# Small tiles allocated together, and fillers so that TensorE's operands start at multiples of 512 bytes

## The chip, the cores and the metric

The kernel runs on one core of one Trainium2 chip. The metric is the device time of one execution in microseconds (us). Of the kernel before, three timed runs are given, with a median of 2034.71 us.

## What is computed

One decoder layer on x of 1024 tokens by 1024 channels: a SwiGLU block (`ffn1`), a token mixer, a second SwiGLU block (`ffn2`) and a final RMS norm. A vector c gives nine sets of 1024 modulation numbers ("mods"), which shift, scale and gate the three blocks:

```python
mod = silu(c) @ w_ada + b_ada;  sh1, sc1, g1, sh2, sc2, g2, sh3, sc3, g3 = split(mod, 9)
x = x + 0.5 * g1 * swiglu(modulate(rms_norm(x), sh1, sc1))      # w_gate, w_up: 1024 x 2816; w_down: 2816 x 1024
x = x + g2 * token_mixer(modulate(rms_norm(x), sh2, sc2))       # w_in 1024 x 4112, SSD heads, pooling, w_out 2048 x 1024
x = x + 0.5 * g3 * swiglu(modulate(rms_norm(x), sh3, sc3))
return rms_norm(x)
```

Everything is float32 outside the chip.

## The kernel before

**The matmul that nearly all time goes into.** Both operands of a large product are split into a high and a low part of type fp32r (`split` at L117 for activations, `prep` at L141 for weights: a rounded copy on ScalarE, the remainder by a subtraction on VectorE). Each product is three matmuls, in `mmw` (L203 to L208): high weights with high activations, high weights with low activations, low weights with high activations. In each, 128 x 128 weights are loaded (the stationary operand) and 512 columns of activations stream past (the moving operand). Every matmul loads its weights anew, also L207, whose weights are those of L206.

**Stages.** `ffn1.phase1` (gate and up products, in Strassen-like combinations), `ffn1.phase2` (down product), two halves of the mixer (`mixer_half(0)` and `(1)`), `ffn2.phase1`, `ffn2.phase2`, and the final norm. In the profiled execution the mixer runs from about 700 to about 1300 us. In it smaller float32 matmuls (128 or 256 columns, L1000 to L1084) ride between the large ones. Weights come in blocks of 128 x 512: SyncE's queue loads them, ScalarE and VectorE split them ahead of use, and a block's buffer is free again when TensorE has read it (`use`, L161; six buffers of kind `w`). The compute engines run their own instruction streams in order; a planner of the tile framework orders the instructions and sets the semaphores.

**Where tiles lie.** A partition of the on-chip memory is filled from both ends. On the left are the constants, up to byte 1152, the pool `sb`, which lives for the whole kernel, and above it the pools of the stage (`ffn1`/`ffn2`, `mixA`, `mix`). On the right, downwards from byte 229344, are the stage's other pools (`ffnB`, `ph2`, `hid`). Within a pool the tiles lie one after another in the order in which they are first asked for, and each is rounded up to 32 bytes. A tile with a tag and `bufs=n` takes n places at once. So a tile of one column (`mod0` to `mod71`, `epsc`, `warm`) takes 32 bytes, and all that comes after is moved by as much. 229344 is 480 more than a multiple of 512, and most tiles of the right are multiples of 512 long. From this the start of each operand of the fp32r matmuls follows. Here it is as the remainder after division by 512 (steps inside a tile, 512 or 2048 bytes, don't change it):

| operand | pool | remainder |
|---|---|---|
| weights `w` (six buffers, from byte 56640) | sb, left | 320 |
| weights `wo` (four buffers) | hid, right | 480 |
| weights `w0` (first group of an ffn) | ffnB, right | 480 |
| `h`, first half in an ffn | ffn, left | 416 |
| `h`, second half and combinations in an ffn | ffnB, right | 480 |
| `h` in the mixer (from byte 103136) | mixA, left | 224 |
| `tw` (spilled products as moving operand) | ph2, right | 480 |
| `yss`, `pl`, `dp` (mixer outputs) | hid, right | 480 |
| `w` as moving operand (first of seven parts of phase 2) | sb, left | 320 |
| `dtw`, 32 or 16 columns of weights, with `h` of the mixer | mixA, left | 224, 352, 480 and 96 |

The trace writes an operand's tile without its number, and `w0` as `w`.

**The tiles that the change touches.** `vec` (parameter columns, L79), `vb` (L94), `epsc` (L106), `warm` (L110), one tile `mod{j}` for each of 72 modulation columns (L622), `aexp` (L865), `halo` and `uhalo` (L876, L877). `ada` (L621 to L634) makes one modulation column: VectorE multiplies a row block by c and accumulates into the column (L623), and ScalarE finishes it in place (L633). Columns 0 to 15 are made at the start; the other 56 during `ffn1.phase1`, one at every second step of the combinations (L837 to L840), and they are read from `ffn1.phase2` on.

Of the kernel before, what the change touches and what calls it, by code (L numbers as in the profile page):

```python
# [7 lines left out]
F32 = mybir.dt.float32  # L8
F32R = mybir.dt.float32r
AF = mybir.ActivationFunctionType  # L10
# [4 lines left out]
P = 128  # L15
# [3 lines left out]
KD = D // P  # L19
# [26 lines left out]
def hybrid_layer(ctx: ExitStack, tc: tile.TileContext, xT, c_bc, wada, vecs, cst,  # L46
                 gu1, dn1, win, wdt, poolw, wout, gu2, dn2, outT):
    nc = tc.nc

    sb = ctx.enter_context(tc.tile_pool(name="sb", bufs=1, side="left"))  # L50
# [25 lines left out]
    cur["t2"] = (cur["ffn"], 9)  # L76


    vec = sb.tile([P, NV], F32, name="vec")  # L79
    cbc = cur["ffn"].tile([P, D], F32, name="cbc", tag="cbc", bufs=1)  # L80
    crow = sb.tile([1, D], F32, name="crow", tag="raw", bufs=4)
    nc.sync.dma_start(out=crow, in_=c_bc)
# [8 lines left out]
    load_x(0)  # L91
    nc.sync.dma_start(out=vec, in_=vecs)
    ones = sb.tile([P, P], F32, name="ones")
    vb = sb.tile([P, 5 * KD], F32, name="vb")  # L94

    def bias_columns():
        for i, (m, n) in enumerate(((1, V_N1), (4, V_NM), (7, V_N2), (2, None), (8, None))):
# [5 lines left out]
                                               op1=ALU.mult)  # L103

    nc.vector.memset(ones, 1.0)
    epsc = sb.tile([P, 1], F32, name="epsc")  # L106
    nc.vector.memset(epsc, EPS)

    def warm_ln():
        t = sb.tile([P, 1], F32, name="warm", tag="warm", bufs=2)  # L110
        i = nc.scalar.activation(out=t, in_=epsc, func=AF.Sqrt)
        tc.keep_in_program_order(i)

# [496 lines left out]
    mods = {}  # L610
# [8 lines left out]
        return raw  # L619

    def ada(j, raw):  # L621
        acc = sb.tile([P, 1], F32, name=f"mod{j}")  # L622
        nc.vector.scalar_tensor_tensor(out=raw, in0=raw, scalar=1.0, in1=cbc, op0=ALU.mult,  # L623
                                       op1=ALU.mult, accum_out=acc)
        m = j // KD
        k = j % KD
        i = {1: 0, 4: 1, 7: 2, 2: 3, 8: 4}.get(m)
        scale = 1.0
        bias = vec[:, V_BADA + j:V_BADA + j + 1]
        if i is not None:  # L630
            bias = vb[:, i * KD + k:i * KD + k + 1]
            scale = 0.5 if i > 2 else vec[:, (V_N1, V_NM, V_N2)[i] + k:(V_N1, V_NM, V_N2)[i] + k + 1]
        nc.scalar.activation(out=acc, in_=acc, func=AF.Identity, scale=scale, bias=bias)  # L633
        mods[j] = acc  # L634


    def rstd(psb, inv_n, n=HT):
# [131 lines left out]
    with tc.manual_schedule(engines={mybir.EngineType.Activation, mybir.EngineType.DVE}):  # L769
# [4 lines left out]
        with tc.manual_schedule(engines={mybir.EngineType.SP}):  # L774
# [5 lines left out]
            ada_pair(3)  # L780
        n1[0].stat.add_pairs([xt[d][0] for d in range(KD)], cb2)
        warm_ln()
        bias_columns()
        for j in (8, 0):
            ada(j, raws[j])
# [16 lines left out]
    for k in range(1, KD):  # L802
        for j in (8 + k, k):
            ada(j, raws[j])
        n1[0].mk(k)
        for b in stream[state["emitted"]:min(14, state["emitted"] + 2)]:
            b.prep()
            state["emitted"] += 1
# [13 lines left out]
    def side1(where, k):  # L822
        if where == "p0":
            if 2 <= k <= 5:
                with tc.high_priority(150):
                    i = 2 * k - 4
                    n1[1].stat.add_pair(i, KD, [xt[i][1], xt[i + 1][1]])
                    if k == 5:
                        n1[1].stat.fin_pairs()
        elif where == "s" and k < 5:  # L830
            for d in ((0, 1), (2, 3), (4, 5), (6,), (7,))[k]:
                n1[1].mk(d)
        elif where == "p1":
            ffn1.spread(k)
        elif where == "s" and 6 <= k < 14:
            ffn1.spread(k + 2)
        elif where == "c" and k >= 14:  # L837
            if ada_next[0] < 72 and k % 2 == 0:
                ada(ada_next[0], ada_raw(ada_next[0]))
                ada_next[0] += 1  # L840
# [19 lines left out]
    mA = cur["mixA"]  # L860
# [1 line left out]
    trs = mA.tile([P, P], F32, name="trs")  # L862
    ident = mA.tile([P, P], F32, name="ident")
    icnt = mA.tile([P, 16], F32, name="icnt")
    aexp = mA.tile([P, 64], F32, name="aexp")  # L865
    dtw = mA.tile([P, KD, 32], F32R, name="dtw")
    open_pool("ph2", "ph2", "right")
    cur["t2"] = (mA, 8)
# [4 lines left out]
    open_pool("hid", "hidp", "right")  # L873
    open_pool("mix", "mix", "left")
    mp = cur["mix"]
    halo = sb.tile([P, 16, 3], F32, name="halo")  # L876
    uhalo = sb.tile([P, KD, 15], F32, name="uhalo")  # L877
    spers = mp.tile([P, G, 2 * P], F32, name="spers")

    def small(nm):  # L880
# [474 lines left out]
```

## Time and profile before

| | |
|---|---|
| three timed runs | 2037.25, 2034.71 and 2033.18 us |
| profiled execution | 2036.55 us, of it 2034.6 us from the first to the last instruction |
| TensorE matmul / weight load busy | 1992.8 us (98%) / 1590.1 us (78%) |
| VectorE / ScalarE / GpSimd busy | 1564.5 us (77%) / 1010.3 us (50%) / 0.2 us |
| DMA | 331.40 MB, mean 163 GB/s |

A matmul's own duration in the trace (some 0.39 us) is longer than the distance from its start to the start of the next, because matmuls overlap in the engine. The cost of one in a row without waits is that distance. A window's count of instructions takes in each that overlaps the window.

### The profile page before, as it was taken

To read this page: it belongs to the slowest core of one execution; us is meant where nothing else is said; L and a number is where in the kernel's file an instruction comes from. 1 tells how busy PE (TensorE), PEld (TensorE's weight loads), DVE (VectorE), ACT (ScalarE), POOL (GpSimd) and SP (SyncE) were. 2 spreads that over 40 slices of the span, in tenths; PEclk is the share of its full clock that TensorE was granted. 3 is DMA by queue.
4 is the path that set the end of the run, shared out by engine and by line. 5 is a ranking of instruction groups with operands and counts; after the bars stand their busy time and mean duration, and the time that the engine had idled before them with its cause. 6 is when DMAs were issued, how large, how long until landed. Compare 5 with 4: busy or idle time off the path is not lost.

```text
span 2034.6 us, 25195 instructions
## 1 busy us (share of the span) xinstructions
PE 1992.8 (98%) x8768; PEld 1590.1 (78%) x8768; DVE 1564.5 (77%) x2559; ACT 1010.3 (50%) x1761; POOL 0.2 (0%) x4
## 2 busy tenths in 40 slices
PE   7999999999999999999999999999999999999996
PEld 4788888887888688888878887768888888878885
DVE  7977887875878867888967998798665565568877
ACT  5744444443444587654467763465434333344442
POOL 0000000000000000000000000000000000000000
PEclk8999999999999999999999999999999999999998
DMA  8365555555887433332332232334332222278783
GB/s 318 103 238 202 191 202 191 194 194 191 298 308 245 145 113 104 126 103 98 115 130 94 94 130 73 97 129 156 136 119 89 102 107 102 83 261 299 234 281 119
DMA packets 155009, 331.40 MB, mean 163 GB/s; under 512 B 16897, under 2 KB 27905, under 8 KB 153858
## 3 DMA queue, kind: packets, MB, share of 16 engines
q1 hardware_dynamic: 154882, 329.80, 47.7%
q8 instruction: 68, 1.11, 0.2%
q14 instruction: 59, 0.48, 0.1%
HBM read 280.91 MB, written 48.82 MB: 162 GB/s over the span
## 4 chain that ended last, share of the span: by engine, by line
PE 82%; DVE 8%; DMA 7%; ACT 1%; issue 1%; SPq 1%; DVEq 0%; ACTq 0%
PE pb L206 26%; PE pb L207 26%; PE pb L208 26%; DMA dw<-in_dn_dram 3%; DMA dth<-sp 2%; DVE w L151 1%; DVE dw L115 1%; PE pb L1084 1%; DVE x L521 1%; DMA araw<-in_wada_dram 1%; DVE ry L642 1%; DVE tw L151 1%; PE pb L1049 1%; PE pb L1078 1%; DVE sq L696 1%
## 5 line engine op out<-in xcount | busy, mean ns | idle before, releaser
L206 PE MATMUL pb<-h,w 128*128 128x512 f32 x1768 | 707.9, 401 | 11.7 <-ACT w L150 11.7
L207 PE MATMUL pb<-h,w 128*128 128x512 f32 x1768 | 702.4, 397 | 0.0
L208 PE MATMUL pb<-h,w 128*128 128x512 f32 x1768 | 701.5, 397 | 0.0
L206 PEld LDWEIGHTS pb<-h,w 128*128 128x128 f32 x1768 | 333.7, 189 | 97.3 <-ACT w L150 15.0
L208 PEld LDWEIGHTS pb<-h,w 128*128 128x128 f32 x1768 | 333.4, 189 | 83.2 <-issue 1.1
L207 PEld LDWEIGHTS pb<-h,w 128*128 128x128 f32 x1768 | 334.1, 189 | 79.7 <-issue 0.7
L151 DVE TENSOR_TENSOR w<-wraw,w 128x512 fp32r<-128x512 f32 x327 | 220.8, 685 | 96.2 <-ACT w L150 95.5
L150 ACT CAST w<-wraw 128x512 fp32r<-128x512 f32 x327 | 200.5, 619 | 181.5 <-PE pb L208 110.6
L206 PE MATMUL pb<-tw,w 128*128 128x512 f32 (+1 forms) x540 | 212.7, 394 | 3.6 <-DVE x L548 3.6
L207 PE MATMUL pb<-tw,w 128*128 128x512 f32 (+1 forms) x540 | 212.1, 393 | 0.0
L208 PE MATMUL pb<-tw,w 128*128 128x512 f32 (+1 forms) x540 | 211.7, 392 | 0.0
L151 DVE TENSOR_TENSOR w<-ws,w 128x512 fp32r<-128x512 f32 x163 | 111.4, 686 | 63.2 <-ACT w L150 63.0
L150 ACT CAST w<-ws 128x512 fp32r<-128x512 f32 x163 | 101.0, 621 | 86.6 <-PE pb L208 82.2
L150 ACT CAST tw<-dth 128x512 fp32r<-128x512 f32 x132 | 81.8, 620 | 118.4 <-DMA dth<-sp 118.2
L150 ACT CAST w<-dw 128x512 fp32r<-128x512 f32 x154 | 94.9, 618 | 73.5 <-DVE dw L115 37.3
L206 PEld LDWEIGHTS pb<-tw,w 128*128 128x128 f32 x540 | 102.2, 189 | 28.1 <-DVE x L548 4.0
L207 PEld LDWEIGHTS pb<-tw,w 128*128 128x128 f32 x540 | 102.2, 189 | 24.2 <-issue 0.5
L208 PEld LDWEIGHTS pb<-tw,w 128*128 128x128 f32 x540 | 102.2, 189 | 23.8
L151 DVE TENSOR_TENSOR w<-dw,w 128x512 fp32r<-128x512 f32 x154 | 105.0, 685 | 14.8 <-ACT w L150 14.6
L151 DVE TENSOR_TENSOR tw<-dth,tw 128x512 fp32r<-128x512 f32 x132 | 90.0, 686 | 30.2 <-ACT tw L150 28.7
L623 DVE SCALAR_TENSOR_TENSOR araw<-araw,cbc 128x1024 f32<-128x1024 f32 x72 | 87.6, 1221 | 30.3 <-DMA araw<-in_wada_dram 29.9
L115 DVE TENSOR_TENSOR dw<-dw 128x512 f32<-128x512 f32 x110 | 75.5, 687 | 33.4 <-DMA dw<-in_dn_dram 32.6
(217 smaller groups left out, 2466.9 us busy)
## 6 DMA issues: line engine op xcount, KB each, us to landing
dw<-in_dn_dram SPq DMA_DIRECT2D x264, 256.0 KB, 4.4
dth<-sp SPq DMA_DIRECT2D x154, 256.0 KB, 4.5
wraw<-in_gu_dram SPq DMA_DIRECT2D x76, 512.0 KB, 3.6
araw<-in_wada_dram SPq DMA_DIRECT2D x72, 512.0 KB, 3.6
wraw<-in_win_dram SPq DMA_DIRECT2D x64, 512.0 KB, 3.4
wraw<-in_wout_dram SPq DMA_DIRECT2D x64, 256.0 KB, 2.7
sp<-u SPq DMA_DIRECT2D x57, 256.0 KB, 2.0
sp<-x SPq DMA_DIRECT2D x57, 256.0 KB, 2.1
```

The source lines that it names most:

```text
L115: nc.vector.tensor_tensor(out=out, in0=a, in1=b, op=op)
L150: nc.scalar.copy(out=self.w[:, 0, :], in_=self.src)
L151: nc.vector.tensor_tensor(out=self.w[:, 1, :], in0=self.src, in1=self.w[:, 0, :].bitcast(F32), op=ALU.subtract)
L206: nc.tensor.matmul(out=out, lhsT=whi, rhs=act[:, 0, c], start=start, stop=False, skip_group_check=True)
L207: nc.tensor.matmul(out=out, lhsT=whi, rhs=act[:, 1, c], start=False, stop=False, skip_group_check=True)
L208: nc.tensor.matmul(out=out, lhsT=wlo, rhs=act[:, 0, c], start=False, stop=stop, skip_group_check=True)
L521: nc.vector.scalar_tensor_tensor(out=xt[d][hf], in0=src, scalar=g[d], in1=xt[d][hf], op0=ALU.mult, op1=ALU.add)
L623: nc.vector.scalar_tensor_tensor(out=raw, in0=raw, scalar=1.0, in1=cbc, op0=ALU.mult, op1=ALU.mult, accum_out=acc)
L642: nc.vector.reciprocal(out=y, in_=y)
L696: nc.vector.tensor_tensor(out=q, in0=q, in1=self.acc, op=ALU.add)
L1049: nc.tensor.matmul(out=b[:, ci * 256:(ci + 1) * 256], lhsT=self.bt[:, c * P:(c + 1) * P], rhs=self.xds[:, c, :], start=True, stop=True)
L1078: nc.tensor.matmul(out=bo[:, s], lhsT=self.prev[:, c, j * P:(j + 1) * P], rhs=cT[:, s], start=True, stop=True)
```

## The change

Small tiles are asked for at the start, one behind another: `vec`, `vb`, `epsc`, `warm`, 16 columns `mod0` to `mod15`, seven tiles of eight columns for the other 56 modulation columns, four accumulators `macc`, `halo` and `uhalo`. With their 32-byte roundings they take 1152 + 160 + 32 + 64 + 512 + 224 + 128 + 192 + 480 = 2944 bytes (`warm` is asked for with 16 columns, one used). From byte 1152 that reaches byte 4096. On the right a pool `edge` with one tile `spare` of 480 bytes lies at the end. `aexp` is asked for with 112 columns, 64 used. Columns 16 to 71 are accumulated in one of the four `macc` tiles in turn, and ScalarE writes the finished column into a column of a shared tile.

```diff
     vec = sb.tile([P, NV], F32, name="vec")
+    vb = sb.tile([P, 5 * KD], F32, name="vb")
+    epsc = sb.tile([P, 1], F32, name="epsc")
+    warm = [sb.tile([P, 16], F32, name="warm")[:, :1]]
+    mod_first = [sb.tile([P, 1], F32, name=f"mod{j}") for j in range(16)]
+    mod_rest = [sb.tile([P, KD], F32, name=f"mods{m}") for m in range(2, 9)]
+    macc = [sb.tile([P, 1], F32, name=f"macc{i}") for i in range(4)]
+    halo = sb.tile([P, 16, 3], F32, name="halo")
+    uhalo = sb.tile([P, KD, 15], F32, name="uhalo")
+    edge = ctx.enter_context(tc.tile_pool(name="edge", bufs=1, side="right"))
+    spare = edge.tile([P, 120], F32, name="spare")
+    nc.gpsimd.memset(spare, 0.0)
...
-    vb = sb.tile([P, 5 * KD], F32, name="vb")
...
-    epsc = sb.tile([P, 1], F32, name="epsc")
...
-        t = sb.tile([P, 1], F32, name="warm", tag="warm", bufs=2)
+        t = warm.pop()
...
-        acc = sb.tile([P, 1], F32, name=f"mod{j}")
+        out = acc = mod_first[j] if j < 16 else macc[j % 4]
+        if j >= 16:
+            out = mod_rest[j // KD - 2][:, j % KD:j % KD + 1]
...
-        nc.scalar.activation(out=acc, in_=acc, func=AF.Identity, scale=scale, bias=bias)
-        mods[j] = acc
+        nc.scalar.activation(out=out, in_=acc, func=AF.Identity, scale=scale, bias=bias)
+        mods[j] = out
...
-    aexp = mA.tile([P, 64], F32, name="aexp")
+    aexp = mA.tile([P, 112], F32, name="aexp")[:, :64]
...
-    halo = sb.tile([P, 16, 3], F32, name="halo")
-    uhalo = sb.tile([P, KD, 15], F32, name="uhalo")
```

## Rows read from the trace of the kernel before

**Rows 1.** The page: busy time of TensorE; the chain that ended last, by engine.

```profile
PE 1992.8 (98%) x8768; PEld 1590.1 (78%) x8768; DVE 1564.5 (77%) x2559; ACT 1010.3 (50%) x1761; POOL 0.2 (0%) x4
PE 82%; DVE 8%; DMA 7%; ACT 1%; issue 1%; SPq 1%; DVEq 0%; ACTq 0%
```

**Rows 2.** Busy time (count) of each engine by window, granted clock, DMA share, GB/s.

```profile
200.00:300.00 100.00, 100.00 (x429) 80.41 (x429) 81.28 (x133) 43.45 (x85) 0.00 (x0) 1.00 0.57 199
...
1100.00:1200.00 100.00, 100.00 (x533) 81.75 (x532) 89.68 (x151) 78.06 (x132) 0.00 (x0) 1.00 0.38 124
...
1300.00:1400.00 100.00, 95.17 (x388) 73.39 (x387) 87.96 (x134) 60.20 (x102) 0.00 (x0) 0.97 0.33 110
```

**Rows 3.** Timeline of TensorE, 1000 to 1027 us: start, duration, line, output and inputs.

```profile
1000.59 0.40 PE L206 MATMUL pb<-pl,wo 128*128 128x512 f32 x1
...
1011.28 0.39 PE L208 MATMUL pb<-pl,wo 128*128 128x512 f32 x1
1011.51 0.39 PE L206 MATMUL pb<-pl,w 128*128 128x512 f32 x1
...
1022.52 0.40 PE L208 MATMUL pb<-pl,w 128*128 128x512 f32 x1
1022.75 0.39 PE L896 MATMUL pb<-h,dtw 128*32 128x512 f32 x1
...
1026.46 0.40 PE L206 MATMUL pb<-h,w 128*128 128x512 f32 x1
```

**Rows 4.** Timeline of TensorE in phase 2 of ffn1, first part.

```profile
496.15 0.39 PE L207 MATMUL pb<-w 128*128 128x512 f32 x1
...
511.79 0.39 PE L207 MATMUL pb<-w 128*128 128x512 f32 x1
```

**Rows 5.** Matmul groups by line and shape: count, busy us, mean ns, idle before.

```profile
L206 PE MATMUL pb<-h,w 128*128 128x512 f32 x1768 | 707.9, 401 | 11.7 <-ACT w L150 11.7
...
L206 PE MATMUL pb<-tw,w 128*128 128x512 f32 x516 | 205.4, 398 | 0.0
...
L206 PE MATMUL pb<-pl,w 128*128 128x512 f32 x96 | 37.6, 405 | 0.0
...
L206 PE MATMUL pb<-w 128*128 128x512 f32 x88 | 34.5, 392 | 0.9 <-ACT w L150 0.9
...
L206 PE MATMUL pb<-yss,w 128*128 128x512 f32 x64 | 25.7, 402 | 0.0
...
L206 PE MATMUL pb<-yss,wo 128*128 128x512 f32 x64 | 25.3, 396 | 0.0
...
L206 PE MATMUL pb<-dp,w 128*128 128x512 f32 x32 | 12.8, 400 | 0.0
...
L206 PE MATMUL pb<-pl,wo 128*128 128x512 f32 x32 | 12.5, 390 | 0.0
...
L789 PE MATMUL pb<-sq,ones 128*128 128x512 f32 x12 | 5.3, 593 | 0.0
```

**Rows 6.** What TensorE waited for: us in total, times, longest.

```profile
PE pb L206 <- ACT w L150: 12.7, 6, 8.1
```

**Rows 7.** Splitting of a weight block, groups by line and shape.

```profile
L151 DVE TENSOR_TENSOR w<-wraw,w 128x512 fp32r<-128x512 f32 x327 | 220.8, 685 | 96.2 <-ACT w L150 95.5
...
L150 ACT CAST w<-wraw 128x512 fp32r<-128x512 f32 x327 | 200.5, 619 | 181.5 <-PE pb L208 110.6 <-issue 50.9 <-DMA wraw<-in_gu_dram 11.3
```

**Rows 8.** Busy time by window where DMA and VectorE are fullest.

```profile
560.00:580.00 20.00, 20.00 (x87) 16.06 (x86) 15.32 (x26) 12.62 (x23) 0.00 (x0) 1.00 0.96 332
...
1120.00:1140.00 20.00, 20.00 (x102) 16.22 (x101) 19.91 (x40) 14.53 (x23) 0.00 (x0) 1.00 0.29 93
```

**Rows 9.** Timeline of TensorE at the start: four float32 matmuls, one behind another.

```profile
16.95 1.88 PE L789 MATMUL pb<-sq,ones 128*128 128x512 f32 x4
```

**Rows 10.** A modulation column's two instructions, groups by line and shape.

```profile
L623 DVE SCALAR_TENSOR_TENSOR araw<-araw,cbc 128x1024 f32<-128x1024 f32 x72 | 87.6, 1221 | 30.3 <-DMA araw<-in_wada_dram 29.9
...
L633 ACT ACTIVATE mod<-mod,vec 128x1 f32<-128x1 f32 x32 | 9.4, 294 | 18.5 <-DVE araw L623 18.4
```

## The prediction

> **What bounds the kernel now.** I read the page's busy times first. TensorE is busy for 98% of the span with 8768 matmuls and as many weight loads [rows 1], while VectorE has 77% and ScalarE 50%, so less work on either of those would buy little. The chain that ended last says the same: 82% of it is TensorE, 8% VectorE, 7% DMA. Next come the windows [rows 2]. From 200 to 300 us TensorE has no idle time, the granted clock is 1.00 (2.4 GHz, the upper of the two levels), and 429 matmuls fall in the window. An instruction that only overlaps the window's edge is counted too, and one lasts some 0.39 us, so the distance from start to start is (100 + 0.39) / 429 = 0.2340 us. Nothing waits there, so this distance is the kernel's price, and what would change it must be in the matmuls themselves.
>
> So I looked for places where the same matmul runs at another distance, and the timeline has one [rows 3]. A single call of `down` runs 48 matmuls with weights from `wo` and then 48 with weights from `w`. Line, shape, moving tiles (`pl`) and clock are the same. The first 48 go from 1000.59 to 1011.28 us: 47 steps, 227.4 ns each. The other 48 go from 1011.51 to 1022.52 us: 47 steps, 234.3 ns each. The reader is to see that only the place of the weights differs: `wo` and `pl` both start at remainder 480, `w` at 320. The second such place is the first part of phase 2, where weights and moving operand both lie in `w` (320 and 320): 69 steps from 496.15 to 511.79 us, 226.7 ns each [rows 4]. My reading is that a step costs 226.7 ns where both operands start at the same remainder modulo 512, and 234 ns where they don't.
>
> **The change part by part.** *Addresses.* By the sizes in the change the small tiles end at byte 4096, so `raw`, `x`, `ones`, `ry` and `w` behind them start at multiples of 512, and `ffn`, `mixA` and `mix` too, since `sb` is then 161 x 512 bytes long. On the right 229344 - 480 = 228864 = 447 x 512. In `mixA` 64 + 448 bytes (`icnt`, `aexp`) make 512, so `dtw` and `h` start at multiples as well. All fp32r operands of L206 to L208 then have remainder 0. It isn't quite "every operand": `ut` (L1127) is 2112 bytes long and shares its tag with the `gt` tiles, so these still go up in steps of 64, and some float32 operands behind them follow. That concerns the small matmuls only, and I count nothing for it.
>
> *What it saves.* Pairs with unequal remainders: `h`,`w` 1768, `tw`,`w` 516, `pl`,`w` 96, `yss`,`w` 64, `dp`,`w` 32 for one line of three, so 3 x 2476 = 7428 matmuls [rows 5]. Equal already: `w` alone 88, `yss`,`wo` 64, `pl`,`wo` 32, so 3 x 184 = 552 [rows 5]. With 234.0 ns [rows 2] going to 226.7 ns [rows 4], 7.3 ns x 7428 = 54.2 us. The 72 matmuls of 256 columns near the end and the 32 with `dtw` add under 0.5 us, and I leave them out.
>
> *What of it is not handed on.* Where TensorE waits for another engine, a faster row of matmuls before it only makes the wait longer. From 1300 to 1400 us 388 matmuls stand where 429 would fit [rows 2], and the waits for `w` copies add up to 12.7 us over the run [rows 6]. I count some 400 matmuls ahead of such waits (about 150 in that window, the rest at the start, between ffn1 and the mixer, and at the end; an estimate from these rows): 400 x 7.3 ns = 3 us. The gain is then 51 us. Its ends: 54 us if all is handed on, and some 41 us if the stretches below give back 10 us.
>
> *Who is late next.* The weights are split ahead of TensorE, and what ends ScalarE's idle time before a copy is mostly TensorE giving a buffer free (110.6 of 181.5 us [rows 7]), so preparation waits for TensorE, not the reverse. Its cost per block (619 ns on ScalarE, 685 ns on VectorE [rows 7]) stands against 12 matmuls, 2.72 us at the new distance. Two places have little room: DMA's share is 0.96 from 560 to 580 us, and VectorE is busy for 19.91 of 20 us from 1120 to 1140 us [rows 8]. In both TensorE had no idle time, and the window of 100 us around the second has VectorE at 89.68% [rows 2]. Speeding TensorE up by 3% asks for 92%. That fits, with some waits where bursts meet. If this cover fails in the mixer (some 600 us, 3% of which are 18 us, less where small matmuls stand), about half of that, 10 us, goes; that is the lower end above.
>
> *The small tiles.* The same instructions run. A column's accumulation on VectorE takes 1.22 us and ScalarE's finish 0.29 us [rows 10], unchanged; only the target of the latter moves. Sharing four accumulators adds a wait: the accumulation of column j must come after ScalarE's read for column j - 4. VectorE's other work is queued behind it, and TensorE waits for that in the end. But columns are made at every second step of the combinations, so four of them span some twenty microseconds, and ScalarE's instruction follows the accumulation directly. Cost 0. If each of 52 waits cost as much as ScalarE's finish, that would be 52 x 0.29 = 15 us of VectorE time in `ffn1.phase1`, where VectorE has 19 us idle in 100 [rows 2], so it would still be hidden. The columns' readers come in later stages. One memset on GpSimd (its four take 0.2 us together [rows 1]) lies on an engine that does nothing else: 0. Moving `halo`, `uhalo`, `vb` and `epsc` changes no instruction.
>
> *A rule that speaks against it.* In rows 3 the place of the weights alone changes the step by 6.9 ns (227.4 and 234.3). The Trainium skill ("TensorE: Matmul & The Clock Gate", "Step-by-step: what each phase is for") says that the weight load and the moving operand have read ports of their own, and that loading the next weights takes no read bandwidth from the running matmul. By that rule the weights' address can't matter and the sum would be 0. The trace doesn't agree, and the measurement decides.
>
> **The rivals.** *Pools, not remainders (no change).* Each fast pair comes from one pool (`w` with `w` in `sb`; `wo` with `yss` and `pl` in `hid`), each slow pair of L206 to L208 from two. If the pool, or the region, is what counts, the change moves all by a few bytes and leaves 2034.7 us. For it: the two readings can't be told apart on those lines. Against it: L896 and L897 take both operands from `mixA`, with unequal remainders in three of four cases, and their 16 steps from 1022.75 to 1026.46 us take 231.9 ns each [rows 3], slower than 226.7 though they load only 32 or 16 columns.
>
> *Multiples of 512 do more than equal remainders.* The four float32 matmuls of 512 columns at the start take 1.88 us [rows 9]; one lasts 593 ns [rows 5], so the starts are (1880 - 593) / 3 = 429 ns apart. If fp32r streams at half that with nothing added, a step is 215 ns, and the gain is 7428 x 19 + 552 x 11.7 ns = 148 us: 1890 us with 3% of it lost to waits. For it: 226.7 isn't the lowest distance one can think of. Against it: the two equal remainders, 320 (a multiple of 64) and 480 (not one), give the same 226.7 to 227.4 ns, so where the pair starts has not mattered so far. The Trainium skill (same page, "Back-to-back issue gap") gives N / 2.4 + 2.5 ns, 216 ns for 512 columns; by it the gain would be an estimate of 140 us. No row of this trace shows an fp32r matmul that fast.
>
> *Another engine takes over.* If preparation in the mixer and in phase 2 can't go 3% faster, the gain is left only in the two phase 1 stages: of the 1768 `h`,`w` in a line 512 are the mixer's (32 projections x 8 x 2 halves), so 1256 of 2476 are left, half the gain: 27 us, 2008 us. For it: rows 8. Against it: the window means.
>
> *Slower: remainder 0 on both sides is the bad pair.* No fp32r pair before has remainder 0. If weights and activations that both start at a multiple of 512 meet at the same place, and each matmul pays as much again as the unequal pair does now (234.0 + 7.3 = 241.3 ns), the 7428 cost 54 us more and the 552 cost 8 us more: 2097 us. It decides for slower once the mean step passes (7428 x 234.0 + 552 x 226.7) / 7980 = 233.5 ns. For it: nothing measured. Against it: equal remainders were the fast case at two places.
>
> **How the numbers follow.** The sum belongs to the profiled execution: span 2034.6 - 51 = 1983.6 us, in an execution of 2036.55 - 51 = 1985.5 us. The median of the three runs lies 1.84 us below the profiled execution, so 2034.71 - 51 = 1984 us is forecast. Chances: equal remainders 0.78 (1975 to 1995), remainder 0 better still 0.06 (1890), half the gain 0.04 (2008), no change 0.08 (2035), slower 0.04 (2097). The range 1968 to 2010 takes in the likeliest case with the 10 us of the unsure covers, and the half gain. Under 0.2% (4 us) a change can't be told from none. Faster is 0.78 + 0.06 + 0.04 = 0.88, within 0.2% 0.08, slower 0.04.
>
> **What would show it.** Right: from 200 to 300 us some 443 matmuls in place of 429 (100.39 / 0.2267), no step in the distance between `pl`,`wo` and `pl`,`w`, the first part of phase 2 as before at 226.7 ns, and the same durations on VectorE and ScalarE. The waits of TensorE grow by a few us, around 1300 us and at the stages' seams. Wrong: 429 again there (the pool reading), 465 or more (remainder 0 does more), 416 (the bad pair), or 443 there but idle time in the mixer's windows (another engine took over). A `mod` column or `macc` among what VectorE waits for would show the added wait.

## The result, and the profile after

The changed kernel takes 1997.86 us (median of 4 runs, 1997.42 to 1999.76) against 2034.84 us of the kernel before on the same chip. The ratio is 0.9819, 95% interval 0.9802 to 0.9836. The forecast was 1984, the range 1968 to 2010: the direction and the mechanism came as predicted, but 14 us of the gain are missing. The profiled execution took 1997.48 us, with a span of 1995.5 us: 39.1 us less than before. Lines have moved by 10 to 12; L206 to L208 are L216 to L218 now.

The page of the changed kernel, busy times and chain, to be held against [rows 1]:

```profile
PE 1945.6 (97%) x8768; PEld 1587.5 (80%) x8768; DVE 1561.6 (78%) x2559; ACT 1007.0 (50%) x1761; POOL 0.4 (0%) x5
PE 71%; DVE 12%; DMA 11%; ACT 2%; issue 2%; SPq 1%; DVEq 0%; ACTq 0%
```

The instructions are the same but for one GpSimd memset. In the chain, 11 points have gone from TensorE, most of them to VectorE and DMA: here the missing gain shows first. The windows, same columns as [rows 2]:

```profile
200.00:300.00 100.00, 100.00 (x442) 82.69 (x441) 84.09 (x139) 44.02 (x88) 0.00 (x0) 1.00 0.57 200
...
1100.00:1200.00 100.00, 98.23 (x514) 81.29 (x512) 90.03 (x154) 69.81 (x120) 0.00 (x0) 1.00 0.35 112
...
1300.00:1400.00 100.00, 94.93 (x398) 75.83 (x399) 93.89 (x150) 61.00 (x104) 0.00 (x0) 0.97 0.44 145
```

The first has 442 matmuls, 443 were forecast. The second had no idle TensorE time before and now has 1.77 us. (By then the two kernels are some 20 us apart, so the same window holds other instructions, and its counts do not compare.) The place of [rows 3] in the changed kernel, TensorE's timeline, 48 matmuls with `wo` and 48 with `w`:

```profile
982.18 0.39 PE L216 MATMUL pb<-pl,wo 128*128 128x512 f32 x1
...
992.84 0.39 PE L218 MATMUL pb<-pl,wo 128*128 128x512 f32 x1
993.06 0.39 PE L216 MATMUL pb<-pl,w 128*128 128x512 f32 x1
...
1003.72 0.39 PE L218 MATMUL pb<-pl,w 128*128 128x512 f32 x1
```

Both halves now take 10.66 / 47 = 0.2268 us a step; the 234.3 ns of [rows 3] are gone. What TensorE waited for, against [rows 6] (total, times, longest; the changed kernel's six largest):

```profile
PE pb L216 <- ACT w L160: 12.5, 5, 7.6
PE pb L216 <- DVE x L558: 6.3, 1, 6.3
PE pb L678 <- DVE sq L673: 3.5, 3, 2.4
PE pb L785 <- ACT crow L782: 3.3, 1, 3.3
PE pb L713 <- DVE sq L708: 3.0, 3, 1.8
PE pb L906 <- ACT h L128: 2.3, 2, 1.8
```

The wait for `w` copies has not grown (12.7 before). The wait for VectorE's update of `x` has (3.6 before), and so have those for `sq` at L708 (0.9 before) and `h` (1.0 before). The preparation of a weight block and of a modulation column, against [rows 7, 10]:

```profile
L161 DVE TENSOR_TENSOR w<-wraw,w 128x512 fp32r<-128x512 f32 x327 | 221.3, 688 | 85.9 <-ACT w L160 83.3 <-PE pb L218 1.7
L635 DVE SCALAR_TENSOR_TENSOR araw<-araw,cbc 128x1024 f32<-128x1024 f32 x72 | 87.7, 1224 | 40.8 <-DMA araw<-in_wada_dram 40.6
```

The other engines' instructions last what they did (685 and 1221 ns before), and VectorE's 72 accumulations wait for DMA alone: the wait that the four shared accumulators add does not appear.

**The account.** Both kernels run the same matmuls in the same order, so their starts can be compared one with one. Of the distances from an fp32r matmul of 512 columns to the next matmul, 7958 changed by 60 ns or less, and together they are 52.6 us shorter. Of all distances 41 changed by more, and together they are 13.0 us longer. By their place in the changed kernel: first 60 us 2.6; 176 to 183 us (ffn1.phase1) 0.8; 482 us (start of phase 2) 0.4; 666 to 692 us (ffn1 to mixer) 2.4; 841 to 1214 us (mixer) 3.3; 1318 to 1334 us 1.0; 1766 us -0.4; the tail from 1963 us 2.7. With 0.3 us of small changes among the rest, 52.6 - 13.0 - 0.3 = 39.3, the span's 39.1 but for rounding and what lies outside the first and the last start.

These are single executions, and the places that give back differ from one to the next. In the profiles of three more kernels at the new pace (the changed one again, and those with remainders 256 and 224 below) the larger changes come to 12.6, 11.0 and 19.2 us, with 3.5 to 3.8 in the mixer, 2.1 to 6.3 in the passage from ffn1 and 1.2 to 4.2 in the tail.

Not all of it comes from the faster pace. The second kernel of the next section has the grouped tiles but the old pace, and the same comparison finds nothing given back in its ffn1.phase1 and mixer, and 1.5 us gained in its passage from ffn1. Its first 60 us, however, are 2.3 us longer than before, nearly as much as the changed kernel's 2.6. There the granted clock tells the kernels apart. Windows from 50 to 60 us, columns as in [rows 2], of the kernel before, the changed one and the one with the old pace:

```profile
50.00:60.00 10.00, 7.55 (x29) 5.13 (x29) 7.90 (x15) 9.04 (x19) 0.00 (x0) 1.00 0.43 152
50.00:60.00 10.00, 7.55 (x22) 4.76 (x21) 7.88 (x14) 8.24 (x17) 0.00 (x0) 0.83 0.47 171
50.00:60.00 10.00, 7.55 (x23) 5.20 (x22) 7.97 (x14) 8.37 (x17) 0.00 (x0) 0.83 0.46 174
```

So some 10 of the 13 us are left for hand-overs that the faster pace met.

Two of these places, followed to the engine that holds them. In the mixer TensorE waits for VectorE's sum `sq`. VectorE's and TensorE's timelines of the changed kernel:

```profile
1172.65 0.69 DVE L1014 TENSOR_TENSOR xds<-pb,dds 128x512 f32<-128x512 f32 x1
1173.25 0.69 DVE L708 TENSOR_TENSOR sq<-sq 128x512 f32<-128x512 f32 x1
...
1171.84 0.39 PE L218 MATMUL pb<-yss,wo 128*128 128x512 f32 x1
1174.00 1.12 PE L713 MATMUL pb<-sq,ones 128*128 128x512 f32 x2 [1.77 <-DVE sq L708]
```

And the same instructions in the kernel before:

```profile
1191.77 0.68 DVE L1004 TENSOR_TENSOR xds<-pb,dds 128x512 f32<-128x512 f32 x1
1192.37 0.68 DVE L696 TENSOR_TENSOR sq<-sq 128x512 f32<-128x512 f32 x1
...
1194.01 0.40 PE L208 MATMUL pb<-yss,wo 128*128 128x512 f32 x1
1194.24 1.02 PE L701 MATMUL pb<-sq,ones 128*128 128x512 f32 x2
```

TensorE's last product ahead of the sum has moved forward by 1194.01 - 1171.84 = 22.2 us, VectorE's sum only by 1192.37 - 1173.25 = 19.1. Before, VectorE was done 1.2 us ahead of TensorE; now it is late. VectorE had 38.83 of 40 us busy up to this point before and has 37.82 of 39 now: with the same instructions and hardly an idle moment it cannot follow.

The tail, VectorE's and TensorE's timelines of the changed kernel:

```profile
1958.19 0.69 DVE L653 TENSOR_SCALAR rv<-pb 128x512 f32<-128x512 f32 x1 [0.96 <-ACT ry L652]
...
1964.36 5.39 DVE L1273 SCALAR_TENSOR_TENSOR o<-x,vec,ry 128x512 f32<-128x512 f32 x8
1969.67 1.66 DVE L558 SCALAR_TENSOR_TENSOR x<-pb,mods,x 128x256 f32<-128x256 f32 x4
...
1970.20 0.58 PE L216 MATMUL pb<-tw,w 128*128 128x256 f32 x1 [6.33 <-DVE x L558]
```

And the first of them in the kernel before:

```profile
1997.38 0.69 DVE L641 TENSOR_SCALAR rv<-pb 128x512 f32<-128x512 f32 x1 [0.96 <-ACT ry L640]
```

From that instruction to the end of the span it is 1995.5 - 1958.19 = 37.3 us now and was 2034.6 - 1997.38 = 37.2 us: the tail has not become faster at all. VectorE's order is norm chain, eight outputs (5.39 us), and only then the residual updates for which TensorE waits. The granted clock has a part in these 37 us. Windows of 20 us of the changed kernel and of the one with the old pace, from that instruction:

```profile
1958.00:1978.00 20.00, 13.67 (x80) 12.38 (x79) 15.61 (x21) 2.33 (x7) 0.00 (x0) 0.83 0.27 105
1993.00:2013.00 20.00, 19.36 (x118) 16.40 (x116) 17.55 (x26) 3.59 (x10) 0.00 (x0) 1.00 0.28 105
```

In the kernel before the clock is 0.83 there too, and TensorE waited 3.56 us for `x`. With the old pace and the grouped tiles VectorE's order is the same, but TensorE, later in that run, waited 0.55 us, the clock stayed at 1.00, and the stretch took 2028.2 - 1993.07 = 35.1 us.

### The profile page after: what moved, and what is told of

Same layout as the page of the kernel before. It is cut to its first block, busy times and chain, and to the rows that moved or that the text cites. A ratio compares the mean times of both kernels' runs of the same rounds, so it can differ in the third digit from the quotient of the medians.

```text
span 1995.5 us, 25196 instructions
## 1 busy us (share of the span) xinstructions
PE 1945.6 (97%) x8768; PEld 1587.5 (80%) x8768; DVE 1561.6 (78%) x2559; ACT 1007.0 (50%) x1761; POOL 0.4 (0%) x5
## 4 chain that ended last, share of the span: by engine, by line
PE 71%; DVE 12%; DMA 11%; ACT 2%; issue 2%; SPq 1%; DVEq 0%; ACTq 0%
PE pb L216 23%; PE pb L218 22%; PE pb L217 22%; DMA dth<-sp 5%; DMA dw<-in_dn_dram 4%; DVE w L161 3%; DVE dw L125 1%; DVE tw L161 1%; DVE x L531 1%; DMA araw<-in_wada_dram 1%; PE pb L1094 1%; DVE ry L654 1%; DVE acr L125 1%; PE pb L713 1%; PE pb L1059 1%
## 5 line engine op out<-in xcount | busy, mean ns | idle before, releaser
L216 PE MATMUL pb<-h,w 128*128 128x512 f32 x1768 | 697.3, 395 | 11.7 <-ACT w L160 11.4
L218 PE MATMUL pb<-h,w 128*128 128x512 f32 x1768 | 690.5, 391 | 0.0
L217 PE MATMUL pb<-h,w 128*128 128x512 f32 x1768 | 690.4, 391 | 0.0
L216 PEld LDWEIGHTS pb<-h,w 128*128 128x128 f32 x1768 | 333.4, 189 | 87.3 <-ACT w L160 15.1
L218 PEld LDWEIGHTS pb<-h,w 128*128 128x128 f32 x1768 | 332.8, 188 | 72.2 <-DVE w L161 1.4
L216 PE MATMUL pb<-tw,w 128*128 128x512 f32 (+1 forms) x540 | 209.0, 387 | 6.3 <-DVE x L558 6.3
L217 PE MATMUL pb<-tw,w 128*128 128x512 f32 (+1 forms) x540 | 208.3, 386 | 0.0
L218 PE MATMUL pb<-tw,w 128*128 128x512 f32 (+1 forms) x540 | 207.9, 385 | 0.0
L216 PEld LDWEIGHTS pb<-tw,w 128*128 128x128 f32 x540 | 102.0, 189 | 27.2 <-DVE x L558 6.7
L218 PEld LDWEIGHTS pb<-tw,w 128*128 128x128 f32 x540 | 101.9, 189 | 20.4
```

The lines of the kernel that those rows point to most:

```text
L216: nc.tensor.matmul(out=out, lhsT=whi, rhs=act[:, 0, c], start=start, stop=False, skip_group_check=True)
L217: nc.tensor.matmul(out=out, lhsT=whi, rhs=act[:, 1, c], start=False, stop=False, skip_group_check=True)
L218: nc.tensor.matmul(out=out, lhsT=wlo, rhs=act[:, 0, c], start=False, stop=stop, skip_group_check=True)
```

## The experiments: which starts are fast

All kernels of this section but the last differ from the changed one in fillers only. The place read is that of [rows 3]: the first and last of the 48 matmuls with `pl` and `w`, `w` on the left side of the memory, `pl` on the right, 47 steps. The steps of `wo` with `pl` are 226.6 to 226.8 ns in each of them.

**All operands at remainder 224.**

```diff
+    lift = sb.tile([P, 56], F32, name="lift")
+    nc.gpsimd.memset(lift, 0.0)
...
-    spare = edge.tile([P, 120], F32, name="spare")
+    spare = edge.tile([P, 64], F32, name="spare")
```

> The changed kernel with fillers that put every fp32r operand of L206 to L208, left and right, at remainder 224 modulo 512 instead of 0. Theory A (a step is short when weights and moving operand have the same remainder, whatever it is): step 226.7 ns everywhere, time as the changed kernel, 1998 us within 4 us, ratio to before 0.982. Theory B (multiples of 512 are what counts): step 234 ns or so, 2030 to 2040 us, ratio 1.00. Theory C (the pools, or the regrouped small tiles, did it): 1998 us as in A, so this run does not part A from C; the run with the old remainders does.

```profile
997.81 0.39 PE L218 MATMUL pb<-pl,w 128*128 128x512 f32 x1
...
1008.46 0.39 PE L220 MATMUL pb<-pl,w 128*128 128x512 f32 x1
```

10.65 / 47 = 226.6 ns, and 2002.11 us, ratio 0.9859 (0.984 to 0.9878). That a start is a multiple of 512 bytes does not matter. That the two have to agree is what the next run shows. The changed kernel itself, run again later, had 0.984 (0.9822 to 0.9858), so the 4 us between this and its first runs tell nothing.

**The grouped small tiles, but the remainders unequal again** (`w` 0, `h` on the left 96, the right side 160).

```diff
-    spare = edge.tile([P, 120], F32, name="spare")
+    spare = edge.tile([P, 80], F32, name="spare")
...
+    gap = sb.tile([P, 24], F32, name="gap")
+    nc.gpsimd.memset(gap, 0.0)
```

> The changed kernel with its grouped small tiles and shared accumulators, but fillers that make the remainders unequal again (w at 0, h on the left at 96, all on the right at 160: the same differences as before, up to a sign). Theory A: step 234 ns, and all of the gain is gone: 2032 to 2037 us, ratio 1.00. Theory C (the regrouping of the small tiles gives the gain, or the pools): 1998 us, ratio 0.98. If grouping has a price of its own (the shared accumulators' wait), the time is above 2037 us; the 3 us that the start lost in the changed kernel would show here as well.

```profile
1011.33 0.39 PE L216 MATMUL pb<-pl,w 128*128 128x512 f32 x1
...
1022.34 0.40 PE L218 MATMUL pb<-pl,w 128*128 128x512 f32 x1
```

11.01 / 47 = 234.3 ns, and 2028.0 us, ratio 0.9982 (0.9973 to 0.9991). All the rest of the change is in this kernel, so grouping, shared accumulators and the other moves are worth some 0.2% (0.1 to 0.3); the remainders make the gain. The time is below the 2032 us that theory A asked for. Its profiled execution is 6.4 us shorter than that of the kernel before, and 5.1 of them are in the tail, where TensorE waited 0.55 us for `x` in place of 3.56; whether the grouping does that stays open.

**The right side half of 512 off (256).**

```diff
-    spare = edge.tile([P, 120], F32, name="spare")
+    spare = edge.tile([P, 184], F32, name="spare")
```

> The changed kernel with the right side moved by 256 bytes: left at 0, right at remainder 256. Pairs on the left (w with h of the left) stay equal, pairs left with right differ by 256. Theory A with modulus 512: 226.7 ns on the left-left pairs, 233 to 234 ns on left-right pairs (tw,w; yss,w; pl,w), 226.7 ns on yss,wo and pl,wo; some 5040 of 7980 matmuls slow, 2020 to 2035 us. A smaller modulus (256, 128 or 64 bytes): 226.7 ns on all, 1998 us. Pool theory: 226.7 ns on all.

```profile
992.85 0.39 PE L216 MATMUL pb<-pl,w 128*128 128x512 f32 x1
...
1003.51 0.39 PE L218 MATMUL pb<-pl,w 128*128 128x512 f32 x1
```

226.8 ns again, one run of 1995.18 us. My reading "modulo 512" was too narrow: starts that differ by 256 are as good as equal ones.

**The right side 128 off.**

```diff
-    spare = edge.tile([P, 120], F32, name="spare")
+    spare = edge.tile([P, 152], F32, name="spare")
```

> As the run before, the right side moved by 128 bytes (remainder 384). Modulus 512 or 256: 233 to 234 ns on left-right pairs, 2020 to 2035 us. Modulus 128 or 64: 226.7 ns on all, 1998 us. Pool theory: 226.7 ns on all.

```profile
1001.01 0.40 PE L216 MATMUL pb<-pl,w 128*128 128x512 f32 x1
...
1011.93 0.39 PE L218 MATMUL pb<-pl,w 128*128 128x512 f32 x1
```

10.92 / 47 = 232.3 ns, one run of 2014.75 us: slow, though by somewhat less than the 233 ns and 2020 us expected. Pools and sides are the same as with 256, so the reading by pools falls too: the pace follows the remainder.

**The right side 32 off.**

```diff
-    spare = edge.tile([P, 120], F32, name="spare")
+    spare = edge.tile([P, 128], F32, name="spare")
```

> The right-hand operands start at remainder 32, the left-hand ones at 0. Theory (a step is fast when both starts agree modulo 256): left-right pairs take 233 to 234 ns, left-left and right-right pairs 226.7; 2015 to 2030 us by one run. Rival (the penalty needs a difference over some size, or falls with it: 128 gave 232.3 to 233.3, 96 and 64 gave 233.3 to 234.2): 227 to 231 ns at 32, about 2000 to 2008 us.

```profile
1007.93 0.39 PE L216 MATMUL pb<-pl,w 128*128 128x512 f32 x1
...
1018.89 0.39 PE L218 MATMUL pb<-pl,w 128*128 128x512 f32 x1
```

(The filler ends the right side at remainder 480, so it lies 32 below a multiple and not above, as the expectation has it; the difference is 32 all the same.) 10.96 / 47 = 233.2 ns, one run of 2021.01 us. The penalty does not shrink with the difference: 32 costs 6.4 ns, 128 costs 5.5, 160 (the second kernel of this section) 7.5 and 256 nothing.

**One pair of three unequal.** Only the low parts of the weights, read by the third matmul, start at 128.

```diff
-    KINDS = {"w": 6, "tw": 8, "wo": 4, "w0": 14}
+    KINDS = {"w": 5, "tw": 8, "wo": 4, "w0": 14}
...
-                self.w = pool.tile([P, 2, HT], F32R, name=k, tag=k, bufs=KINDS[k])
+                wide = HT + 32 * (k == "w")
+                self.w = pool.tile([P, 2, wide], F32R, name=k, tag=k, bufs=KINDS[k])[:, :, :HT]
```

> The low parts of the weights in the tiles w start at remainder 128 (modulo 256), the high parts and all moving operands at 0; for the room, w has five buffers in place of six, so that only the steps are to be read and not the total. Theory A (a running stream collides with the load of the next weights): the weights of L218 are loaded while L217 streams, so the steps from L217 to L218 take 232 to 233 ns, and those from L216 to L217 and from L218 to the next L216 take 226.7. Theory B (a stream is slow with its own weights): the steps from L218 to the next L216 take 232 to 233 ns, the other two 226.7. Theory C (any unequal pair delays all): all three above 228. By A or B some 2650 steps cost 6 ns each: about 2014 us, more if the fifth buffer is missed.

```profile
1005.87 0.39 PE L217 MATMUL pb<-pl,w 128*128 128x512 f32 x1
...
1016.73 0.39 PE L219 MATMUL pb<-pl,w 128*128 128x512 f32 x1
```

10.86 / 47 = 231.1 ns on the mean. Taken apart over the whole run by the starts in the trace, the step from first to second matmul is 227.1 ns (2333 steps), from second to third 232.5 (2361), from third to the next first 233.9 (2404). Theories A and B had one slow step each; there are two, the step before the matmul with unequal weights and its own. In a row of unequal pairs the two do not add: each step costs 7 ns, not 13. So one unequal pair of three costs 227.1 + 232.5 + 233.9 - 3 x 226.7 = 13.4 ns, nearly as much as two in a row. What in the engine does it stays open. The one run took 2025.52 us; the fifth buffer's part in that was not separated.

## The experiments: where the gain goes

**The changed kernel again**, as the measure for the two below.

> The changed kernel once more, as the measure for the two kernels beside it. 1998 us, ratio to the kernel before 0.982.

2001.0 us (1997.02 to 2003.15, 5 runs), ratio 0.984 (0.9822 to 0.9858); TensorE's wait for `x` 5.4 us in its profile.

**Some outputs behind the residual updates.**

```diff
     def parts2(c):
+        for k in range(0, 5) if c.start == 0 else range(5, KD):
+            store(0, k)
...
-            for k in range(KD):
-                store(0, k)
```

> The eight instructions that make the first half's output (5.39 us on VectorE) stand ahead of the last residual updates in the changed kernel; here only some of them do (one before each update, two more at the start, three behind). Theory (VectorE's queue holds the tail, so that TensorE's faster pace can't be handed on there): TensorE's wait for the update of x falls from 6.3 us to some 4 us, the second norm chain starts 2 to 3 us earlier, and the kernel takes 1995 to 1996 us against 1998. Rival (the tail is set by the norm chain's length or by TensorE): no change, 1998 us.

1995.96 us (1992.51 to 2000.61), ratio 0.9818 (0.9797 to 0.9838), not told apart from the kernel beside it by the times. The profile tells more. What TensorE waited for in the tail:

```profile
PE pb L699 <- ACT sq L698: 3.5, 1, 3.5
```

The wait for `x` is gone and a new one, for ScalarE's squares, has come in its place, since TensorE's order still had the sums of the first half ahead of the second half's matmuls. From the first instruction of the norm chain (1962.98 us) to the end of the span (1996.6 us) it is 33.6 us, against 37.4 us in the kernel beside it (1995.4 - 1957.99). The tail is 3.8 us shorter, as the theory wants and the rival does not; this run's profile had lost 5 us earlier. (The granted clock over its first 20 us is 0.91, against 0.83, so part of the 3.8 us is the clock's.)

**The updates first.**

```diff
-                                nc.vector.scalar_tensor_tensor(out=t, in0=bs[j][:, c], scalar=g[4 + j], in1=t,
-                                                               op0=ALU.mult, op1=ALU.add)
+                                with tc.high_priority(200):
+                                    nc.vector.scalar_tensor_tensor(out=t, in0=bs[j][:, c], scalar=g[4 + j], in1=t,
+                                                                   op0=ALU.mult, op1=ALU.add)
```

> The same instructions, but the residual updates are given a higher priority, which puts them between the outputs on VectorE and moves TensorE's matmuls of the second half ahead of the sums of the first. Theory (VectorE's queue holds the tail): TensorE has nearly no wait for x before its matmuls, VectorE's idle time in the last 40 us (4.1 and 1.8 us in the changed kernel) shrinks, and the kernel takes about 1994 us against 1998. Rival (tail set elsewhere): 1998 us. If the sums of the first half, now behind more matmuls, come too late, it is slower than 1998.

1992.21 us (1990.57 to 1996.22), ratio 0.9801 (0.9783 to 0.9818). VectorE's and TensorE's timelines:

```profile
1957.01 0.69 DVE L654 TENSOR_SCALAR rv<-pb 128x512 f32<-128x512 f32 x1 [0.96 <-ACT ry L653]
...
1963.18 1.41 DVE L1274 SCALAR_TENSOR_TENSOR o<-x,vec,ry 128x512 f32<-128x512 f32 x2
1964.51 0.48 DVE L559 SCALAR_TENSOR_TENSOR x<-pb,mods,x 128x256 f32<-128x256 f32 x1
...
1965.05 0.38 PE L216 MATMUL pb<-tw,w 128*128 128x256 f32 x1 [3.15 <-DVE x L559]
```

The first update stands behind two outputs, not eight, and TensorE waits 3.15 us in place of 6.33 (nearly none was expected). From the norm chain's start to the end it is 1990.3 - 1957.01 = 33.3 us. This version is the fastest of those that compute the whole function, and its interval lies below that of the changed kernel beside it (0.9822 to 0.9858). So another order on VectorE shortens TensorE's wait and makes the tail some 4 us shorter. The wait and the clock (0.91 over the first 20 us here, 0.83 beside it) changed together, and their shares are not told apart: with the old pace the old order took 35.1 us at a clock of 1.00.

**VectorE relieved in the mixer by GpSimd.**

```diff
-            nc.vector.tensor_tensor(out=self.w[:, 1, :], in0=self.src, in1=self.w[:, 0, :].bitcast(F32),
-                                    op=ALU.subtract)
+            (nc.gpsimd if k == "wo" else nc.vector).tensor_tensor(
+                out=self.w[:, 1, :], in0=self.src, in1=self.w[:, 0, :].bitcast(F32), op=ALU.subtract)
```

> The subtraction that makes the low part of a wo block goes from VectorE to GpSimd: 24 blocks, 24 x 0.69 = 16.5 us less for VectorE, four of them (2.6 us) between 1158 and 1163 us, ahead of the sum for which TensorE waits 1.77 us at 1174 us. Theory (VectorE's full queue is what gives the gain back inside the mixer): that wait is gone, TensorE's order and pace stay, VectorE's other durations stay, and the kernel takes 1995 to 1997 us against 1998. Rival (something else sets that wait, ScalarE or the products before it): the wait stays within 0.3 us and the time at 1998. If GpSimd is slow at this (over some 3 us a block) or holds VectorE up, new waits for wo show on TensorE and the time is over 1998.

2001.69 us (1997.6 to 2003.98), ratio 0.9847 (0.9825 to 0.9868): nothing gained. TensorE's wait, and VectorE beside GpSimd:

```profile
1180.03 1.12 PE L713 MATMUL pb<-sq,ones 128*128 128x512 f32 x2 [1.57 <-DVE sq L708]
...
1159.28 3.94 POOL L161 TENSOR_TENSOR wo<-wraw,wo 128x512 fp32r<-128x512 f32 x3 [180.81 <-ACT wo L160]
...
1159.13 0.21 DVE L975 SCALAR_TENSOR_TENSOR cv<-halo,vec,cv 128x1 f32<-128x1 f32 x1
1160.78 1.23 DVE L975 SCALAR_TENSOR_TENSOR cv<-halo,vec,cv 128x2 f32<-128x2 f32 x1
```

The wait fell from 1.77 to 1.57 us only, which is the rival's forecast, but the run can't decide: while GpSimd worked, a VectorE instruction of 0.21 us took 1.23, another 0.84, so part of the relief was lost at once. Elsewhere it did harm: TensorE's waits for this sum and its like came to 7.7 us in all, against 3.0 in the changed kernel. The Trainium skill ("SBUF — State Buffer", "Who interferes with whom") says that only the port pair shared by VectorE and GpSimd causes such contention and that it works as an exclusive lock; the stretched instruction agrees with it.

**The same work left out altogether.**

```diff
+    class High:
...
+        def __getitem__(self, i):
+            return self.t[i[0], 0, i[2]]
...
-            nc.vector.tensor_tensor(out=self.w[:, 1, :], in0=self.src, in1=self.w[:, 0, :].bitcast(F32),
-                                    op=ALU.subtract)
+            if k == "wo":
+                self.w = High(self.w)
+            else:
+                nc.vector.tensor_tensor(out=self.w[:, 1, :], in0=self.src, in1=self.w[:, 0, :].bitcast(F32),
+                                        op=ALU.subtract)
```

> The subtractions for the low parts of the 24 wo blocks are left out, and the third matmul of these blocks takes the high part again; nothing is moved to another engine. VectorE has 16.5 us less to do, 2.6 us of it just ahead of the sum for which TensorE waits 1.77 us at 1174 us in the changed kernel. Theory (VectorE's full queue sets that wait): it is gone or under 0.3 us, with TensorE's steps as they are. Rival (ScalarE or the products before it set it, as the run with GpSimd may say, where VectorE had 0.92 us to wait for a copy): it stays over 1.2 us. The total, by one run, is 1994 to 1998 us in the first case and 1997 to 2002 in the second.

The kernel leaves out the low parts of these weights, so it doesn't compute the layer any more; it serves the reading of the wait alone.

```profile
1168.97 0.69 DVE L718 TENSOR_TENSOR sq<-sq 128x512 f32<-128x512 f32 x1 [1.56 <-ACT sq L716]
...
1169.72 1.13 PE L723 MATMUL pb<-sq,ones 128*128 128x512 f32 x2 [0.97 <-DVE sq L718]
```

The wait falls to 0.97 us, between both forecasts. VectorE is done 1.56 us early and then waits for ScalarE's square: the theory holds for the first 0.8 us, the rival for the rest. Elsewhere in the mixer the same relief took 0.8, 0.9 and 0.6 us at 841, 898 and 1214 us by the starts compared with the changed kernel, 3.0 us with this place, nearly the whole 3.3 that the mixer had given back. The one run took 1988.93 us, below either forecast; 3.8 us of that are a shorter tail, which the edit does not touch and which differs from run to run.

## Why the prediction was right, and where it was not

- *The price of a matmul, and its saving*: right. 7.3 ns on 7428 matmuls were forecast, 54.2 us; 52.6 us were measured on the pace, 7.1 ns a matmul. The count by tiles held, and so did the signs named for it (442 for 443 matmuls, no step between `wo` and `w`).
- *Equal remainders modulo 512*: the right cause with too large a modulus. 256 is enough, by the third experiment.
- *What of it is not handed on*: the step that was mis-sized. 3 us were forecast, from 400 matmuls ahead of waits that existed already; 13.0 us were measured. The method counted only waits visible before. But half of the 13.0 (the mixer, the passage from ffn1 and 0.8 us in ffn1.phase1, 6.6 us) lies where TensorE had hardly a wait and the other engine was just in time: VectorE was 1.2 us early at the mixer's sum and is now 1.8 us late. Another 2.7 lie in the tail, where the wait existed but was priced at far less, and the 2.6 at the start came largely with a fall of the clock, which the sum has no term for and the old pace shows as well. The waits for `w`, on which the estimate was built, did not grow.
- *Who is late next*: half right. Weight preparation kept up, as said. VectorE's fullness in the mixer was seen [rows 8] and 10 us were priced as the lower end; the mixer gave back 3.3. The tail (2.7), the passage into the mixer (2.4) and the first 60 us (2.6) together gave more, and these had only their share of the 3 us above. The lower end of 41 us is by chance near the measured 39.1.
- *Small tiles, added wait, memset*: 0, as forecast; the second experiment puts them at 0.2%, on the faster side.
- *The rivals*: pools fell with the fourth experiment, multiples of 512 as such and remainder 0 as the bad pair with the changed kernel's own 226.8 ns and the first experiment. "Another engine takes over" is true in part: not half the gain but some 10 of 52.6 us.
- *The rule weighed in the prediction* (the Trainium skill, "TensorE: Matmul & The Clock Gate", "Step-by-step: what each phase is for": the weight load takes no read bandwidth from the running matmul): the runs are against what was drawn from it, that the weights' address can't matter. With the same instructions, the place of the operands alone moves a step from 226.8 to 234.3 ns. What in the engine does it, bandwidth or something else, no run here shows.

Shown by runs are the cause of the pace, and that VectorE's order lengthens the tail. The mixer's part is shown by the timelines and in part by the last run. The passage from ffn1 to the mixer was read only: VectorE's norm chain came 13.0 us earlier there (688.47 and 675.45 us), TensorE's last products 14.9. In the first 60 us the loss goes with the clock, but why the clock falls in some kernels and not in others was not tried.

## What to carry to other kernels

When one matmul form runs at two paces in one trace, compare where its operands lie before looking for waits; for fp32r, starts that agree modulo 256 bytes were the fast ones, and a filler of some hundred bytes is all it costs. When the bounding engine gets faster everywhere, list, for each hand-over, how early the other engines are today: what they lack there is given back, though no wait shows yet. Compare with more than one profile, since such places differ from one execution to the next. Then look for work in their queues that nobody waits for, and put it behind what is waited for.

## What the runs showed of the hardware that was not expected

- A stream of 512 fp32r columns takes 226.7 ns a step with the remainders 0, 224, 320 or 480 alike; no pair ran faster. Starts that differ by 32, 128 or 160 bytes modulo 256 take 232 to 234 ns, and a difference of 256 costs nothing.
- One matmul of three with unequal weights slows two steps of three.
- A wait of the same length cost TensorE its clock in one kernel and not in the other. In the changed kernel the granted clock is 0.83 from 50 to 60 us, a mean between its two levels (1.2 and 2.4 GHz), and 1.00 there before. The two sums after the 2.45 us wait took 2.04 us in place of 1.12, though that wait is the same in both; so part of the 2.6 us at the start is the clock's and no wait's. In the kernel with the old pace the clock is 0.83 there too, so the faster pace is not needed for it. The changed kernel:

```profile
54.17 2.04 PE L678 MATMUL pb<-sq,ones 128*128 128x512 f32 x2 [2.45 <-DVE sq L673]
```

- GpSimd's subtraction of 128 x 512 took 1418 ns on the mean of 24, twice VectorE's 688, and lengthened VectorE's instructions beside it.
